# RWKV-7 / HGRN2 mixer layer on one core: another order of the input projections, a longer hold on whole-array visits, and residual tiles asked for later

## The chip, the cores and the metric

The kernel runs on one core of one Trainium2 chip. The metric is the device time in microseconds (us) of one execution, here a median over several runs. The engines that matter are TensorE (PE, with its weight loads shown as PEld), VectorE (DVE), ScalarE (ACT), GpSimd (POOL), and SyncE (SP), whose queue issues nearly all the transfers between HBM and the on-chip memory.

## The reference

One layer on 512 frames of 2048 channels. One input projection feeds two groups of heads: an RWKV-7 recurrence (16 heads of 64) and an HGRN2 gated linear recurrence (8 heads of 128). Their gated outputs are joined, go through one output projection, and the residual is added before a layer norm. Cut to what matters:

```python
proj = jnp.einsum('btd,dc->btc', h, w_in[l])              # 512 x 2048 by 2048 x 8320
rw = _token_shift(proj[..., :RWKV_COLS], shift_mu[l])     # r, k, v, z, and two ranks of 64
hg = proj[..., RWKV_COLS:]                                # q, f, i, z of HGRN2
# RWKV-7, frame by frame, per head (S is 64 x 64):
S = S * w_t + (S @ a_t) b_t^T + v_t k_t^T;   o_t = S @ r_t
# HGRN2, chunks of 64 frames, per head (S is 128 x 128):
S = S * exp(b_last) + k_dec^T i;   o = att(q, k, decay) i + (q * exp(b)) S
y = jnp.einsum('btc,cd->btd', jnp.concatenate([o_rwkv, o_hgrn], -1), w_out[l])
h = _layer_norm(ALPHA * h + y, ln_w[l], ln_b[l])
```

All is float32, and the output has to be float32-like too.

## The kernel before

**Precise matmuls.** Every operand of the two big projections is split into a high and a low part of type fp32r, and each product is made of three matmuls (high by high, high by low, low by high) into the same PSUM bank. This is `three`; its matmuls are the lines L525 of the profile, and L1390 for the first three units. Below, such a matmul of 512 moving columns is called a main matmul. The split of a weight tile `wr` (or `t`, where tiles of that pool hold weights) is one ACT copy (`wh<-wr`) and one DVE subtraction (`wl<-wr,wh`).

**Units.** The input projection is cut into units named by a letter and a number: `w0` (the two ranks), `r`, `k`, `v`, `z` 0 to 7 for RWKV-7 (two heads each), `q`, `f`, `g` 0 to 7 and `i` 0 and 1 for HGRN2 (`g` is its gate). A table, `ORDER`, sets in which order they are computed; `_layout` lays out the weights in the same order. The file holds two tables under that name, and the later one counts.

**The planner.** All other work is written as Python generators that yield operations, each with its engine, reads and writes. While the program is being built, the class `Plan` keeps an estimated clock for every engine. After each main matmul, `pump` goes through its queues of generators, and places an operation in the instruction stream as soon as the estimate says that its inputs will be there. What comes out is a fixed order on each engine; on the chip each engine follows its own order and waits on semaphores. The planner's constants therefore move instructions, and nothing of them runs on the chip.

TensorE does two kinds of work beside the main matmuls, and an interruption of the main stream by such work is called a visit here. A *whole* visit uses the full 128x128 array with float32 operands (the steps of the RWKV scan, `mix<-bd,q` and `mix<-zz,q`, two matmuls each; the outputs of HGRN2 heads; transposes). A *narrow* visit uses parts of the array (16 to 48 matmuls of 32x32 up to 64x128). Each float32 matmul of a visit has two records in the trace. `HOLD` says how long the planner keeps an operation of each kind back, from the moment that it could go, in the hope that a second one joins it; in the last six units (`HURRY`) nothing is held.

**The output projection.** Its first column block (d = 0) runs as rows: for each of 16 k-tiles, four token tiles into the four `main` banks. When those four sums are done, `row_out` adds the residual (`q<-g,main`, DVE), for which `residual` fetches a tile of x into one of four buffers `g` (`g<-x_r`, SP queue). The middle blocks (d = 1 and 2) are then computed by seven *joint passes* of 8 k-tiles and two banks each, a Strassen-like scheme: the first two passes take their weights from `w_all`, later ones partly from sums prepared earlier (`sums_w`, `sums_a`). The weights of a pass come in four loads, two of 512 KB into `wr` and two pairs of 256 KB tiles into `t`. A load into a buffer is issued when the split of what the buffer held is placed, so it waits for that split. The last block (d = 3) follows. The residual tiles of the four blocks stand in one queue, `fetches`, in the order in which `residual` is called: four for d = 0 during the rows, eight for the joint passes, four for d = 3.

Of the kernel before, what the change touches and what calls it, by code (L numbers as in the profile page):

```python
# [39 lines left out]
ORDER = (  # L40
# [3 lines left out]


ORDER = (
# [3 lines left out]


def _order():

    return [(u[0], int(u[1:])) for u in ORDER.split()]
# [10 lines left out]
class Plan:  # L65
# [4 lines left out]

    AFTER = {"pe": 0.2, "act": 0.145, "dve": 0.13, "pool": 0.06, "dma": 0.0, None: 0.1}
    TO_PE = 0.12
    HOLD = {"whole": 0.3, "narrow": 1.0}
    TURN = 0.215
    REST = 1.5
    LEAD = -0.35
# [130 lines left out]
    def worth(self, op, now):  # L207
# [8 lines left out]
        kept = [t for t, o in self.waiting.values() if o.mode[0] == op.mode[0]]  # L216
        if len(kept) == 1 and now < kept[0] + self.HOLD[op.mode[0]]:
            return False
# [44 lines left out]
def mixer_kernel(ctx, tc, head, x_r, w_all, par, up, ln_wb, consts, hmask, out):  # L263
    nc = tc.nc
    pe, sc_e, dve, pool = nc.tensor, nc.scalar, nc.vector, nc.gpsimd
# [9 lines left out]
    def nm(s):  # L275
        uid[0] += 1
        return f"{s}{uid[0]}"
# [5 lines left out]
    plan = Plan({**BUFS, **PBUFS})  # L283
    tags = {}

    def st(tag, shape, dt=F32):
        return spool.tile(shape, dt, tag=tag, name=nm(tag), bufs=BUFS[tag])

    def take(tag, shape=(P, T), dt=F32):

        if not plan.free(tag):
            raise RuntimeError(f"no room: {tag}")
        slot = min(plan.slots[tag])
        plan.slots[tag].remove(slot)
        if tag in PBUFS:
            t = ppool.tile(list(shape), dt, tag=tag, name=nm(tag), bufs=PBUFS[tag])
            plan.banks.add(t.tensor.name)
        else:
            t = st(tag, list(shape), dt)
        name = t.tensor.name  # L300
        plan.busy[name] = (slot[1], None)
        tags[name] = tag
        return t
# [26 lines left out]
    def send(o, i, cost=0.44):  # L330

        nc.sync.dma_start(o, i)
        (to, _), (at, by) = (d.get(ap.tensor.name, (0.0, None)) for d, ap in ((plan.busy, o), (plan.ready, i)))
        plan.clock["sp"] = max(plan.clock["sp"], plan.clock["pe"], to + 0.1, at + 0.1) + cost


    def size(ap):
        n = 1
        for s in ap.shape[1:]:
            n *= s  # L340
        return n
# [160 lines left out]
    def ready(i, home=None):  # L502

        if i < 2 * nload and i not in parts:
            parts[i] = home() if home else tuple(st(t, [P, QT], F32R) for t in ("wh", "wl"))
            if not home:
                ring.append(i)
                before = ring[-1 - BUFS["wh"]] if len(ring) > BUFS["wh"] else -1
                for t in parts[i]:
                    plan.busy[t.tensor.name] = (over.get(before, 0.0), "pe")  # L510

            def run():
                yield from split(*parts[i], raws[i // 2][i % 2])
                whole_parts.add(i)
                if i % 2:
                    load(i // 2 + (2 if i // 2 < joint else 4))

            plan.add(splits, run())

    def three(ps, lh, ll, rh, rl, first, last):  # L520
        n = size(rh)
        for i, (l, r) in enumerate(((lh, rh), (lh, rl), (ll, rh))):
            plan.clock["pe"] += n / 2400 + 0.0145 + plan.turn(("main",))
            plan.mode = ("main",)
            pe.matmul(ps, l, r, start=first and i == 0, stop=last and i == 2)  # L525
            plan.pump()
        if last:
            plan.ready[ps.tensor.name] = plan.busy[ps.tensor.name] = (plan.clock["pe"], "pe")
# [6 lines left out]
    def part(i, width):  # L535

        ready(i)
        for k in range(len(over), min(i, last_parts)):
            over[k] = plan.clock["pe"]
        hi, lo = parts[i]  # L540
        plan.until(lambda: i in whole_parts and by_now(lo))
        return (hi.rearrange("p (k c) -> p k c", c=width), lo.rearrange("p (k c) -> p k c", c=width))

    def main_ps(tags=("main",)):

        def test():
            now = plan.clock["pe"]
            free = [t for t in tags if plan.free(t) and min(plan.slots[t])[1] + 0.15 <= now]
            if not free and plan.free("mix", 3) and sorted(plan.slots["mix"])[0][1] + 0.15 <= now:
                free = ["mix"]  # L550
            return free

        plan.until(test)
        return take(min(test(), key=lambda t: min(plan.slots[t])[1]))
# [891 lines left out]
    asked, whole = [], []  # L1446
# [87 lines left out]
    def union_done(n):  # L1534

        now = plan.clock["pe"]
        for t in {t.tensor.name: t for t in (homes[n, m] for m in range(NPAIRS))}.values():
            plan.busy[t.tensor.name] = (now, "pe")
        if n in ("S2", "S4"):
            drop(*(homes[n, m] for m in range(NPAIRS)))  # L1540
        else:
            drop(homes[n, 0, "ia"], homes[n, 4, "zz"], homes[n, 6, "zz"])
        homes[n, "free"] = True
# [11 lines left out]
    SS = [{} for p in range(NPAIR)]  # L1555

    HURRY = _order()[-6:]
    HS = [{} for _ in range(NHEAD)]
    for name, j in _order()[1:]:
# [195 lines left out]

    xrs = {}

    fetches = plan.queue()

    def residual(t, d):  # L1760
        def run():
            yield lambda: len(whole) == KT and plan.free("g")
            xr = take("g")
            send(xr, x_r[t, :, d * T : d * T + T])
            plan.fetched(xr, 4 * T)
            xrs[t, d] = xr
            now = plan.clock["pe"]
            yield lambda: plan.clock["pe"] > now + (2.0 if d else 0.5)

        plan.add(fetches, run())  # L1770
# [101 lines left out]
    def factor(name, m, i):  # L1872
        sl = slice(i * P, i * P + P)
        if name in ("A11", "A12", "A22"):
            k = korder[2 * m + (name != "A11")]
            sl = slice(T // 2 + i * P, T // 2 + i * P + P) if name == "A22" else sl
            return gh[k][:, sl], gl[k][:, sl]
        plan.until(lambda: (name, m) in unioned and by_now(unioned[name, m][1]))
        hi, lo = unioned[name, m]
        return hi[:, sl], lo[:, sl]  # L1880
# [11 lines left out]
    def home(i):  # L1892
        n = i - single0
        if n < 0:
            if (i - parts0) % 4 < 3:
                return None

            def kept():
                if not fourth:
                    fourth.extend(take("ksq", (P, QT), F32R) for _ in range(2))  # L1900
                for t in fourth:
                    plan.busy[t.tensor.name] = (over.get(i - 4, 0.0), "pe")
                return tuple(fourth)

            return kept
        if n < 7:
            return lambda: tuple(take("t", (P, QT), F32R) for _ in range(2))
        if n < 9:
            def one():
                z = take("zz", (P, 2, QT), F32R)  # L1910
                return z[:, 0], z[:, 1]

            return one
        if n < 11:
            def both():
                if "last" not in homes:
                    homes["last"] = take("ia", (P, 4, QT), F32R)
                return homes["last"][:, 2 * (n - 9)], homes["last"][:, 2 * (n - 9) + 1]

            return both  # L1920
        if n == 11:
            return lambda: tuple(fourth)
        if n == 12:
            return lambda: tuple(take(tag, (P, QT), F32R) for tag in ("pf", "ksq"))

    def prepared(i):

        ready(i, home(i))

    for p, (_, name) in enumerate(PASSES):  # L1930
        pss = []
        for m in range(NPAIRS):
            n = parts0 + p * NPAIRS + m
            hi, lo = part(n, T)
            for i in range(2):
                if m == 0:
                    pss.append(main_ps(banks))
                prepared(n + 1 + 2 * i)
                if i == 0:
                    prepared(n + 2)  # L1940
                three(pss[i], *factor(name, m, i), hi[:, 0], lo[:, 0], m == 0, m == NPAIRS - 1)
                if m == NPAIRS - 1:
                    plan.add(evacs, gather(name, i, pss[i]))
        if name in ("S1", "S2", "S3", "S4"):
            union_done(name)
# [175 lines left out]
```

## Time and profile before

| | |
|---|---|
| median of 3 runs | 1015.25 us (1014.25 to 1015.29) |
| the profiled execution | 1015.2 us, span 1013.3 us |
| granted TensorE clock | 1.000 |
| PE / PEld / DVE / ACT / POOL busy, share of the span | 99% / 82% / 85% / 50% / 4% |
| DMA | 161.74 MB, mean 160 GB/s |

Some rows of the profile show starts and durations of single instructions. Because matmuls are pipelined, a main matmul has a duration of 0.39 us in such a row while the next one starts 0.227 us after it: the distance between starts is what a matmul costs, and the chain of work that ended last gives that distance as the length of a piece divided by its count (x64 in 14.53 us). A number in brackets at the end of a row is the idle time of the engine before it, with what ended it.

### The profile page before, as it was taken

How to read it: one execution, taken by the hardware profiler on the slowest of the kernel's cores; microseconds unless marked ns; L12 is line 12 of the kernel's file. 1: busy time of each engine (PE TensorE's matmuls, PEld its weight loads, DVE VectorE, ACT ScalarE, POOL GpSimd, SP SyncE). 2: the span in 40 equal slices, each digit the busy share in tenths (PEclk: the TensorE clock that was granted, in tenths of full speed). 3: DMA queues.
4: the chain of work that ended last, by engine and by line, in shares of the span. 5: the costliest groups of instructions: out<-in, count | busy, mean ns of one | idle time of the engine just before them, and what ended most of it. 6: DMA issues, size and time to landing. Idle time of an engine off the chain costs nothing.

```text
span 1013.3 us, 18890 instructions
## 1 busy us (share of the span) xinstructions
PE 1006.2 (99%) x7081; PEld 831.2 (82%) x7081; DVE 864.2 (85%) x1894; ACT 507.1 (50%) x963; POOL 43.0 (4%) x78
## 2 busy tenths in 40 slices
PE   9999999999999999999999999999999999999997
PEld 8888888888888888888888888888888888878886
DVE  7688689967898998888989987888999898988867
ACT  5557335345646434544673455636343556466531
POOL 0000000000010001002000010020001001000001
PEclk9999999999999999999999999999999999999999
DMA  9766664442456353235555332346463338797633
GB/s 337 240 215 209 216 225 134 138 136 80 145 145 183 104 150 100 64 100 148 154 172 162 114 91 84 90 139 171 137 186 116 117 104 254 222 308 236 204 126 127
DMA packets 80492, 161.74 MB, mean 160 GB/s; under 512 B 11408, under 2 KB 38288, under 8 KB 80400
## 3 DMA queue, kind: packets, MB, share of 16 engines
q1 hardware_dynamic: 79968, 159.61, 51.5%
q8 instruction: 56, 0.92, 0.4%
q10 hardware_dynamic: 432, 0.92, 0.3%
q14 instruction: 36, 0.29, 0.1%
HBM read 130.48 MB, written 30.02 MB: 158 GB/s over the span
## 4 chain that ended last, share of the span: by engine, by line
PE 99%; DVE 0%; ACT 0%; DVEq 0%; issue 0%
PE main L525 75%; PE mix L354 10%; PE mix L525 9%; PE main L1390 3%; PE main L354 2%; PE mix L1341 0%; PE mix L359 0%; PE main L1984 0%; DVE wl L378 0%; ACT wh L368 0%; DVE inv L391 0%; DVEq L2117 0%; DVE inv L1339 0%
## 5 line engine op out<-in xcount | busy, mean ns | idle before, releaser
L525 PE MATMUL main<-xl,wh 128*128 128x512 f32 x848 | 333.3, 393 | 0.0
L525 PE MATMUL main<-xh,wl 128*128 128x512 f32 x848 | 333.1, 393 | 0.0
L525 PE MATMUL main<-xh,wh 128*128 128x512 f32 x848 | 332.9, 393 | 0.0
L368 ACT ACTIVATE wh<-wr 128x512 fp32r<-128x512 f32 x285 | 177.9, 627 | 168.4 <-PE main L525 118.8
L378 DVE TENSOR_TENSOR wl<-wr,wh 128x512 fp32r<-128x512 f32 x285 | 193.9, 681 | 27.8 <-ACT wh L368 23.9
L525 PEld LDWEIGHTS main<-xh,wl 128*128 128x128 f32 x848 | 159.4, 188 | 32.5
L525 PEld LDWEIGHTS main<-xh,wh 128*128 128x128 f32 x848 | 159.3, 188 | 32.4
L525 PEld LDWEIGHTS main<-xl,wh 128*128 128x128 f32 x848 | 159.3, 188 | 32.2
L525 PE MATMUL main<-wh,xh 128*128 128x512 f32 x194 | 76.1, 392 | 0.0
L378 DVE TENSOR_TENSOR inv<-inv 128x256 f32<-128x256 f32 (+10 forms) x184 | 64.4, 355 | 13.7 <-DMA inv<-w_all 10.3
L525 PE MATMUL main<-wh,xl 128*128 128x512 f32 x194 | 76.0, 392 | 0.0
L525 PE MATMUL main<-wl,xh 128*128 128x512 f32 x194 | 75.9, 391 | 0.0
L525 PEld LDWEIGHTS main<-wh,xh 128*128 128x128 f32 x194 | 36.4, 188 | 8.1 <-DVE t L391 0.5
L525 PEld LDWEIGHTS main<-wl,xh 128*128 128x128 f32 x194 | 36.4, 188 | 7.4
L525 PEld LDWEIGHTS main<-wh,xl 128*128 128x128 f32 x194 | 36.5, 188 | 7.4
L378 DVE TENSOR_TENSOR inv<-inv,inv 64x30 f32<-64x30 f32 (+14 forms) x120 | 38.5, 321 | 2.7
L368 ACT ACTIVATE t<-mix 64x128 f32<-64x128 f32 (+3 forms) x71 | 18.4, 262 | 41.0 <-DVE zz L378 24.0
L378 DVE TENSOR_TENSOR t<-t,tot 128x256 f32<-128x256 f32 x96 | 37.9, 416 | 0.3
L369 ACT ACTIVATE t<-main,om 128x512 f32<-128x512 f32 x33 | 22.2, 685 | 29.7 <-PE main L525 22.7
L391 DVE SCALAR_TENSOR_TENSOR bd<-mix,pc,bd 64x64 f32<-64x64 f32 x112 | 31.7, 283 | 5.3 <-PE mix L354 3.0
L368 ACT ACTIVATE q<-t 128x256 f32<-128x256 f32 (+1 forms) x51 | 21.8, 445 | 24.9 <-DVE t L378 21.4
L369 ACT ACTIVATE t<-main 128x512 f32<-128x512 f32 x31 | 17.9, 594 | 22.8 <-PE main L525 22.6
(320 smaller groups left out, 1614.8 us busy)
## 6 DMA issues: line engine op xcount, KB each, us to landing
wr<-w_all SPq DMA_DIRECT2D x142, 512.0 KB, 3.9
inv<-w_all SPq DMA_DIRECT2D x16, 512.0 KB, 5.1
sums_w<-inv SPq DMA_DIRECT2D x16, 512.0 KB, 5.0
q<-head SPq DMA_DIRECT2D x14, 448.0 KB, 5.8
far<-ksq SPq DMA_DIRECT2D x22, 256.0 KB, 4.0
t<-w_all SPq DMA_DIRECT2D x20, 256.0 KB, 4.5
t<-spill SPq DMA_DIRECT2D x17, 256.0 KB, 3.9
far<-q SPq DMA_DIRECT2D x8, 512.0 KB, 5.0
```

Of the source, the lines that this page charges most:

```text
L354: return Op([("pe", cost, lambda: pe.matmul(o, l, r, start=start, stop=stop, **kw))], [l, r], [o], mode=("narrow", l.shape[0], 32 if m <= ...
L368: return "act", cost, lambda: sc_e.activation(o, i, f, scale=scale)
L369: return "act", cost, lambda: sc_e.activation(o, i, f, scale=scale, bias=bias)
L378: return dve_op([a, b], o, lambda: dve.tensor_tensor(o, a, b, f), base=base or 0.16 if o.shape[0] < P and size(o) == C and o.tensor.name i ...
L391: return dve_op([a, b], o, lambda: dve.scalar_tensor_tensor(o, a, s, b, f1, f2), per=0.00113, base=0.085 if o.shape[0] == P and size(o) > ...
L525: pe.matmul(ps, l, r, start=first and i == 0, stop=last and i == 2)
L1390: pe.matmul(pss[a], *ops, start=k == 0 and low == of == 0, stop=k == KT - 1 and low == 1)
```

## The change

Four edits:

1. A new `ORDER` table behind the others.
2. `HOLD["whole"]` goes from 0.3 to 1.0: outside of the last six units, the planner keeps a whole visit back for up to 1 us, as it did with narrow ones.
3. In `three`, the planner's clock is charged 0.09 for a main matmul that follows a whole visit.
4. The residual tiles of d = 1 and 2 are asked for only when the planner's clock stands 8 us behind the start of the joint passes; until then they were asked for as soon as a buffer `g` was free.

```diff
+ORDER = (
+    "w0 k0 r0 f1 r1 k1 v0 g0 v1 q1 q0 f0 g1 i0 z0 z1 r3 k2 f2 r2 "
...
-    HOLD = {"whole": 0.3, "narrow": 1.0}
+    HOLD = {"whole": 1.0, "narrow": 1.0}
...
     def three(ps, lh, ll, rh, rl, first, last):
         n = size(rh)
         for i, (l, r) in enumerate(((lh, rh), (lh, rl), (ll, rh))):
-            plan.clock["pe"] += n / 2400 + 0.0145 + plan.turn(("main",))
+            plan.clock["pe"] += n / 2400 + 0.0145 + plan.turn(("main",)) + (0.09 if plan.mode[0] == "whole" else 0.0)
...
-    fetches = plan.queue()
+    fetches, began = plan.queue(), []

     def residual(t, d):
         def run():
             yield lambda: len(whole) == KT and plan.free("g")
+            if 0 < d < 3:
+                yield lambda: bool(began) and plan.clock["pe"] > began[0] + 8.0 and plan.free("g")
...
         ready(i, home(i))

+    began.append(plan.clock["pe"])
     for p, (_, name) in enumerate(PASSES):
```

The kernel computes the same things with the same instructions; 5500 matmuls stand on TensorE before and after, of the same kinds. Their order is another one from the fourth unit on. Three places follow. In all of them the number behind a tile's name only tells buffers apart, and the lines of the new kernel lie six further down.

**SP, around the start of the joint passes.** Before, from the first residual tile on (`g` is a residual tile; `wr` and `t` from `w_all` are weights of the first two joint passes):

```order
L332 DMA g_9527<-x_r 128x512
L332 DMA g_9533<-x_r 128x512
L332 DMA g_9550<-x_r 128x512
L332 DMA g_9557<-x_r 128x512
L332 DMA t_9553<-w_all 128x512
L332 DMA t_9554<-w_all 128x512
L332 DMA wr_9582<-w_all 128x1024
L332 DMA t_9574<-w_all 128x512
L332 DMA t_9575<-w_all 128x512
L332 DMA g_9600<-x_r 128x512
L332 DMA wr_9615<-w_all 128x1024
L332 DMA g_9624<-x_r 128x512
```

After, the same stretch of the queue:

```order
L338 DMA t_9539<-w_all 128x512
L338 DMA t_9540<-w_all 128x512
L338 DMA g_9560<-x_r 128x512
L338 DMA wr_9570<-w_all 128x1024
L338 DMA g_9572<-x_r 128x512
L338 DMA t_9543<-w_all 128x512
L338 DMA t_9544<-w_all 128x512
L338 DMA g_9592<-x_r 128x512
L338 DMA g_9603<-x_r 128x512
L338 DMA wr_9612<-w_all 128x1024
L338 DMA t_9539<-w_all 128x512
L338 DMA t_9540<-w_all 128x512
```

The first pair of `t` tiles has moved ahead of all residual tiles, the second pair has two of them ahead of it where it had four, and the first residual tile of the joint passes has gone from the tenth place here to behind the four `t` loads that follow.

**DVE, at the same place.** Before, with `q<-g,main` the residual addition of the d = 0 rows, `wl<-wr,wh` and `ksq<-wr` the splits of the first joint pass (`wl_9539` is its first k-tile, `wl_9577` its second):

```order
L378 TENSOR_TENSOR wl_9539<-wr_9455,wh_9538 128x512
L378 TENSOR_TENSOR t_9525<-t_9526,g_9266 128x256
L378 TENSOR_TENSOR t_9526<-g_9415,t_9525 128x256
L391 SCALAR_TENSOR_TENSOR q_9559<-g_9527,main_8964 128x512
L1732 BN_STATS stats<-q_9559 128x6
L378 TENSOR_TENSOR wl_9577<-wr_9455,wh_9576 128x512
L391 SCALAR_TENSOR_TENSOR q_9561<-g_9533,main_8974 128x512
L391 SCALAR_TENSOR_TENSOR q_9563<-g_9550,main_8986 128x512
L378 TENSOR_TENSOR wl_9593<-wr_9512,wh_9592 128x512
L378 TENSOR_TENSOR ksq_9607<-wr_9512,ksq_9606 128x512
```

After (`wl_9566` is the second k-tile of the first pass, `wl_9585` the third, `ksq_9600` the fourth):

```order
L384 TENSOR_TENSOR wl_9566<-wr_9455,wh_9565 128x512
L384 TENSOR_TENSOR t_9558<-g_9065 128x256
L384 TENSOR_TENSOR t_9558<-t_9559,g_9065 128x256
L384 TENSOR_TENSOR t_9559<-g_9414,t_9558 128x256
L384 TENSOR_TENSOR wl_9585<-wr_9510,wh_9584 128x512
L384 TENSOR_TENSOR t_9589<-tw_9314,t_9589 128x256
L384 TENSOR_TENSOR ksq_9600<-wr_9510,ksq_9599 128x512
L397 SCALAR_TENSOR_TENSOR q_9548<-g_9560,main_8983 128x512
L384 TENSOR_TENSOR wl_9618<-t_9539,wh_9617 128x512
```

The splits of the second to fourth k-tile now stand ahead of the first residual addition, which waits for its tile of x; before, three residual additions stood ahead of the third.

**PE, in the d = 0 rows.** Before, the outputs of the last RWKV scan (`big`) and a visit of the last HGRN2 pair (`q`, `t`) stand together:

```order
L525 MATMUL main_8986<-wh_8940,xl_8897 128x512
L354 MATMUL mix_9017<-zz_7679,big_7306 64x64 x16
L354 MATMUL mix_9018<-zz_8005,big_7306 64x64 x16
L354 MATMUL mix_9069<-q_8173 32x32 x8
L354 MATMUL mix_9069<-q_8174 32x32 x8
L354 MATMUL mix_9069<-t_8055,t_8151 64x64 x4
L354 MATMUL mix_9069<-t_7846,t_7954 64x64 x4
L525 MATMUL main_8995<-wh_8940,xh_8896 128x512
```

After, the outputs stand alone:

```order
L531 MATMUL main_8999<-wh_9036,xh_9078 128x512
L360 MATMUL mix_9142<-zz_7687,big_7266 64x64 x16
L360 MATMUL mix_9143<-zz_8295,big_7266 64x64 x16
L531 MATMUL main_8999<-wl_9037,xh_9078 128x512
L531 MATMUL main_8999<-wh_9036,xl_9079 128x512
```

The other visit now stands ahead, between main matmuls of the last unit. Over the whole program, counted in this way, visits made of whole-array matmuls alone went from 60 to 53. Narrow matmuls of two different steps share a visit in four places before: 32x32 ahead of the 128x32 kind twice, the other way round once, and the one just shown. After, there are three: the first kind once, the second twice.

2 rows, old and new, of the table ORDER are left out of this document.

## Prediction

> **What bounds the kernel now.** I read the chain of work that ended last first, by line:
>
> ```profile
> PE main L525 75%; PE mix L354 10%; PE mix L525 9%; PE main L1390 3%; PE main L354 2%; PE mix L1341 0%; PE mix L359 0%; PE main L1984 0%; DVE wl L378 0%; ACT wh L368 0%; DVE inv L391 0%; DVEq L2117 0%; DVE inv L1339 0%
> ```
>
> Nearly the whole span is TensorE working through its own stream. Next the busy time by stretch (length, then PE, PEld, DVE, ACT, POOL with instruction counts, the clock, the DMA engines' busy share, GB/s), for the projections and for the hand-over from the d = 0 rows to the joint passes:
>
> ```profile
> 40.00:868.00 828.00, 827.88 (x6308) 686.70 (x6307) 719.50 (x1613) 420.17 (x799) 36.62 (x63) 1.00 0.49 144
> 868.00:895.00 27.00, 26.09 (x113) 20.54 (x112) 22.68 (x48) 13.55 (x30) 0.00 (x0) 1.00 0.82 258
> ```
>
> In the projections TensorE is never idle for longer than the pipeline hides, the clock is full, and the matmuls are the same after the change. So a new order can win there only what visits cost beside their matmuls, and short waits. The second stretch is different: TensorE idles, and the DMA engines are 0.82 busy against 0.49. Its chain, with the price of a main matmul first (14.53 / 64 = 0.227 us):
>
> ```profile
> 87.17 14.53 PE main L525 x64
> ...
> 880.58 8.41 PE mix L525 x36
> 888.99 0.63 ACT wh L368
> ...
> 889.64 0.70 DVE wl L378
> ...
> 890.39 4.76 PE mix L525 x19
> ```
>
> From 880.58 to 895.15 are 14.57 us. The chain names 36 + 19 matmuls, and one more (by high, low) runs between the ACT and the DVE piece: 56 x 0.227 = 12.71. So 1.86 us are lost, nearly all where TensorE stands still for the split of the seventh k-tile of the first pass. The instructions behind it, by start:
>
> ```profile
> 879.61 0.69 DVE L391 SCALAR_TENSOR_TENSOR q<-g,main 128x512 f32<-128x512 f32 x1 [1.39 <-DMA g<-x_r]
> 880.94 0.67 DVE L378 TENSOR_TENSOR wl<-wr,wh 128x512 fp32r<-128x512 f32 x1
> 881.64 0.33 SPq L332 DMA_DIRECT2D wr<-w_all  x1
> 882.06 0.86 SPq L332 DMA_DIRECT2D t<-w_all  x2
> 888.98 0.63 ACT L368 ACTIVATE wh<-t 128x512 fp32r<-128x512 f32 x1 [2.75 <-PE mix L525]
> ```
>
> DVE waits 1.39 us for a residual tile and only then does the split of the second k-tile (880.94 to 881.61). The load `wr<-w_all` on SP needs that split (its buffer), and goes at 881.64; the pair `t<-w_all` stands behind it on SP and goes at 882.06. ACT starts on that pair at 888.98, 6.9 us later. The row names TensorE as what ended the wait, but TensorE itself was waiting; that it was the landing is my inference, and these rows of the issues, the first over the whole run, the second for 874 to 884 us, support it:
>
> ```profile
> t<-w_all SPq DMA_DIRECT2D x20, 256.0 KB, 4.5
> ...
> t<-w_all SPq DMA_DIRECT2D x4, 256.0 KB, 6.1
> ```
>
> So the loss has two causes in a row: a load that goes late because DVE's queue stands behind a residual tile, and a slow landing because residual tiles and weights share busy DMA engines.
>
> **The change, part by part.**
>
> *Residual tiles later, and the new place of the splits: -1.86 us.* In the new DVE order the splits of the second to fourth k-tile stand ahead of the first residual addition. That takes away the wait of 1.39 us and the 1.33 us from the addition's start to the split's (880.94 - 879.61), so up to 2.7 us; ACT's half of the split has to come first, so I count 2.0. The `wr` load moves by as much, and the second `t` pair behind it too, less one residual tile that now stands between them on SP (half of 0.86 us): issued at 880.5. With even the slow 6.1 us it lands at 886.6; ACT and DVE take 0.63 + 0.70 to split it, 887.9, and TensorE needs it at 888.8 (36 matmuls behind 880.58): 0.9 us of slack where there was a deficit, and 2.5 with the usual 4.5 us. Fewer bytes stand ahead of it, too: two residual tiles instead of four, and the first `t` pair goes earlier. Ends: all 1.86 us gained; nothing gained. I take the whole. The joint passes' own residual tiles come later; up to the fourth pass a sum leaves its PSUM bank before the residual is added, so only DVE's queue can wait for them.
>
> *Whole visits, 60 to 53.* A visit of two matmuls (four records), one of ten, and the main matmuls around them:
>
> ```profile
> 243.94 1.81 PE main L525 x8
> 245.76 0.44 PE mix L354 x4
> 246.20 1.60 PE main L525 x7
> ...
> 466.24 2.23 PE mix L354 x20
> 468.47 2.77 PE mix L525 x12
> ```
>
> Without 15 x 0.227 = 3.405 for the main matmuls, the short visit costs 3.85 - 3.405 = 0.445, and the long one 2.23 + 2.77 - 12 x 0.227 = 2.28, or 0.455 for every two matmuls. A fixed cost of coming and going would make the short one dearer by the matmul; it does not, and by the rounding of these rows it lies between -0.01 and 0.01 us. Seven visits fewer bring -0.07 to +0.07, taken 0. The 0.09 us that the planner is now charged for each return is not in this trace. The longer hold alone costs TensorE nothing, since main matmuls fill the time; what it delays is a rival.
>
> *Narrow visits parted: +0.28.* Alone, a 32x32 visit, a 128x32 visit, and both in one in either order:
>
> ```profile
> 391.86 0.68 PE mix L354 x50
> 392.54 2.72 PE main L525 x11
> 395.26 1.50 PE mix L354 x114
> 396.76 4.10 PE main L525 x17
> ...
> 148.12 0.82 PE mix L354 x64
> 148.94 8.15 PE main L525 x35
> ...
> 778.91 1.62 PE mix L354 x114
> 780.53 4.31 PE main L525 x18
> ```
>
> Without 0.227 for each main matmul behind them: 0.90 and 1.03 alone, 1.74 with 32x32 first (saves 0.19), 1.84 the other way round (saves 0.09). The third kind of sharing, scan outputs with the 128x32 and 128x64 kinds, is priced by these:
>
> ```profile
> 278.12 2.02 PE mix L354 x64
> 280.13 18.81 PE main L525 x82
> ...
> 173.10 1.00 PE mix L354 x48
> 174.10 26.07 PE main L525 x114
> ...
> 832.40 3.02 PE mix L354 x112
> 835.42 14.74 PE main L525 x64
> ```
>
> 2.22 and 1.19 alone, 3.23 together: saves 0.18. Before: 2 x 0.19 + 0.09 + 0.18 = 0.65. After: 0.19 + 2 x 0.09 = 0.37. The change loses 0.28.
>
> *Other waits of the old order: 0.* The new order cannot keep the places of the old short waits, but it has new ones of its own. The largest before lie around 828 us, where a visit waits for DVE and the rows then wait for their fourth PSUM bank:
>
> ```profile
> 827.10 0.62 PE mix L354 x4
> 827.72 1.17 PE main L525 x5
> ...
> 828.92 2.11 PE main L525 x8
> ```
>
> The visit: 0.62 - 0.44 = 0.18. Behind it, from 827.72 to 831.03 are 3.31 us for 13 main matmuls, 0.36 more than 13 x 0.227. Together 0.54 us; with the shorter ones elsewhere I put them at 0.9 (an estimate: two thirds as much again). The same planner with the same margins made the new order, so I expect as much again: ends -0.9 and +0.9, taken 0.
>
> *Sum.* 1015.2 (the profiled execution: its span of 1013.3 and 1.9 around it; 0.05 below the median of the runs) - 1.86 + 0 + 0.28 + 0 = 1013.6 us. 0.2% is 2.0 us, about what a measurement of this kernel can tell from no change, so "faster" begins at 1013.2.
>
> **Rivals.**
>
> 1. *The wait stays, or moves to the third pass.* Four residual tiles (1 MB) now go while `sums_w` and `sums_a` tiles are fetched for it.
>
> ```profile
> 894.18 0.33 SPq L332 DMA_DIRECT2D wr<-sums_w  x1
> ...
> wr<-sums_w SPq DMA_DIRECT2D x8, 512.0 KB, 4.6
> ...
> 904.22 22.09 PE main L525 x96
> ```
>
> The pass's first weights go at 894.18, land 4.6 us later and are split in 1.3, 900.1; the pass starts at 904.22, so 4.1 us are spare. All of 1 MB ahead of them at 258 GB/s takes 4.1 us: just covered, if it all lay ahead. The Trainium skill ("DMA: Bandwidth & Descriptors", section "Issuing engines are not separate DMA queues") says that transfers run on the same 16 engines and interleave, whichever engine starts them: by that, deferring tiles moves load and removes none, and this kernel could lose in pass three what it wins in pass one. The row of 0.82 busy engines agrees that they are shared; that the slack is used up, no row shows. With the gain gone: 1015.2 + 0.28 = 1015.5.
>
> 2. *The scattered waits go as well.* In the new order two visits instead of one, and the same nine main matmuls, stand between the last unit's end and the first matmul into the fourth bank, which gives its evacuation 0.45 us more. Against it: nothing in the trace says that the other waits do not come again. 1013.6 - 0.9 = 1012.7.
>
> 3. *Slower: the hold stretches the RWKV scans.* Between the two visits of a scan step the old order has 7 main matmuls (as in the row of 246.20), the new one 10 in the unhurried groups: 0.68 us for each of 7 steps, 4.8 us for a scan. If the buffers of a scan then come free so late that the next group's evacuation stops and the four main banks fill, TensorE waits for up to that long once: 1013.6 + 4.8 = 1018.4. It decides from 3.7 us of new waits on (1017.3). Against it: the last group's visits are not held, and the new order has its last scan's outputs 69 matmuls later but the last transposes of HGRN2 31 and 18 earlier, ahead of the rows that need them.
>
> 4. *A return from a whole visit does cost the 0.09.* Seven fewer: -0.63, so 1013.0. The visits above speak against it.
>
> **How the numbers follow.** My forecast's case (the wait of the first pass gone, other waits about as before) has 0.60; its own range is 1012.9 to 1014.4, a third of it under 1013.2. Rival 1 has 0.15 (same), rival 2 0.17 and rival 4 0.02 (faster), rival 3 0.06 (slower by more than 2.0 us in 0.05). Faster: 0.20 + 0.17 + 0.02 = 0.39. Slower 0.05. Same 0.56. The range goes from rival 2 less 0.2 (1012.5) up to 1015.0, where rival 1 begins if a part of the wait comes back: that leaves out most of rival 1, rival 3, and little else.
>
> **What would show it.** In the chain of the new kernel, no ACT or DVE piece between 880 and 895 us; the second `t` pair issued about 2 us earlier; DVE without an idle stretch on `g<-x_r` ahead of the second split. Visits of two matmuls still at 0.45 us. The 32x32 and 128x32 visits alone at 0.90 and 1.03. The forecast is wrong if such a piece stands in the third pass, or if TensorE's busy share in the projections falls below 827.9 of 828 us.

## The result, and the profile after

The changed kernel is slower: 1030.8 us median of 4 runs (1026.9 to 1033.2) against 1015.3 (1014.3 to 1016.1) for the kernel before, a ratio of 1.015 with a 95% interval of 1.013 to 1.017. That is 15.5 us, where I had forecast a gain of 1.7. The profiled execution is the longest of the four: 1033.24 us, with a span of 1031.5, 18.2 more than before. The runs also scatter over 6.3 us, those of the kernel before over 1.8. The lines of `mixer_kernel` stand six lower in the changed file: L531 here is L525 before, L360 is L354, L384 is L378, L397 is L391.

Two lines answer the first two of before. The first is the page's chain by line, the second the busy time by stretch (length, then PE, PEld, DVE, ACT, POOL, the clock, the DMA engines' busy share, GB/s):

```profile
PE main L531 62%; PE mix L360 9%; PE mix L531 5%; PE main L1396 3%; DMA inv<-w_all 3%; DVE wl L384 2%; DMA sums_w<-inv 2%; PE main L360 1%; DMA wr<-w_all 1%; DVE inv L384 1%; DVE t L384 1%; DMA g<-x_r 1%; DMA t<-far 1%; DMA spill<-g 0%; DMA t<-spill 0%
...
40.00:868.00 828.00, 818.17 (x6233) 675.60 (x6232) 711.74 (x1611) 405.29 (x760) 34.82 (x61) 0.99 0.46 137
```

The chain had hardly anything in it but TensorE; now 8% of it are transfers, `inv<-w_all` first. TensorE's busy time in the projections is 818.2 of 828 us instead of 827.9, and the clock is no longer full throughout. This is the sign that the prediction named for being wrong.

To size the loss I took the starts of neighbouring matmuls of 512 columns (0.227 us apart when nothing waits) and summed what was over it, from 20 us on. Gaps of 0.35 us and more ("holes" below) hold 15.3 us, against 2.6 before; main matmuls at 0.427 us (half speed) add 3.8, against none. Together 16.5 us more, of 18.2. Two places hold 11 us of it. The first, at 95 us, by start on PE and on DVE, then the transfers issued from 86 to 98 us (KB each, median us to landing):

```profile
95.02 0.39 PE L531 MATMUL main<-xl,wh 128*128 128x512 f32 x1
98.92 0.79 PE L531 MATMUL main<-xh,wl 128*128 128x512 f32 x1 [3.51 <-DVE wl L384]
```

```profile
96.91 1.34 DVE L384 TENSOR_TENSOR inv<-inv 128x256 f32<-128x256 f32 x3 [6.03 <-DMA inv<-w_all]
98.17 0.69 DVE L384 TENSOR_TENSOR wl<-wr,wh 128x512 fp32r<-128x512 f32 x1
```

```profile
wr<-w_all SPq DMA_DIRECT2D x1, 512.0 KB, 5.8
q<-far SPq DMA_DIRECT2D x4, 128.0 KB, 6.4
inv<-w_all SPq DMA_DIRECT2D x1, 512.0 KB, 7.0
sums_w<-inv SPq DMA_DIRECT2D x1, 512.0 KB, 7.8
```

TensorE stands because it needs the low half `wl` of a weight tile. That split is an easy 0.69 us on DVE, and its operands had been there; but it stands in DVE's queue behind three subtractions of `weight_sums`, and these wait 6.0 us for their `inv` tile. The tile took 7.0 us to land, behind five other transfers issued in the 2.6 us ahead of it and with a store right behind. The planner reckons 1.8 us behind the transfer itself (`fetched`), and counts there neither the four `q<-far` tiles nor the store into `sums_w`.

When TensorE went on, it ran at half speed. Two stretches behind the two longest holes (the number behind POOL's count is the granted clock):

```profile
99.00:104.60 5.60, 5.60 (x13) 4.37 (x14) 3.84 (x8) 0.99 (x2) 0.00 (x0) 0.50 0.80 240
...
170.00:173.40 3.40, 3.40 (x10) 2.67 (x9) 3.37 (x3) 0.90 (x2) 0.00 (x0) 0.52 0.04 16
```

So the place at 95 us costs 3.9 us of idling and 13 x 0.2 us of slow matmuls. The second place, at 166 us, has the same beginning; its chain:

```profile
156.20 5.75 DMA inv<-w_all
...
163.69 0.69 DVE wl L384
...
166.55 0.68 DVE wl L384
...
168.16 0.69 DVE t L397
...
168.88 3.42 PE main L531 x9
```

It costs 2.9 us and seven slow matmuls. The waits of DVE on these tiles in the whole run, before and after (us in total, times, longest):

```profile
DVE inv L378 <- DMA inv<-w_all: 10.3, 6, 3.9
```

```profile
DVE inv L384 <- DMA inv<-w_all: 20.5, 7, 6.0
```

The row of before was there to be read: DVE already stood 3.9 us behind such a tile, and nothing of it reached TensorE. I had looked at TensorE's waits, not at this near miss.

The rest of the loss is spread: 1.4 us at 140 and 1.3 at 335, 0.8 at 727 and at 794, and 1.4 at 886 in the rows just ahead of the joint passes, where an output of the last heads, turned by way of DRAM (`far`), comes back late (chain):

```profile
875.41 4.44 DMA wr<-w_all
879.87 6.17 DMA t<-far
...
886.16 0.88 DVE g L397 x3
```

### The profile page after: what moved, and what is told of

The parts are those of the page before. It is cut to its first block, busy times and chain, and to the rows that moved or that the text cites. A ratio compares the mean times of both kernels' runs of the same rounds, so it can differ in the third digit from the quotient of the medians.

```text
span 1031.5 us, 18880 instructions
## 1 busy us (share of the span) xinstructions
PE 1013.1 (98%) x7081; PEld 832.6 (81%) x7081; DVE 871.6 (85%) x1922; ACT 500.3 (49%) x937; POOL 46.7 (5%) x78
## 4 chain that ended last, share of the span: by engine, by line
PE 82%; DMA 8%; DVE 7%; issue 1%; ACT 1%; POOL 0%; SPq 0%; DVEq 0%; POOLq 0%; ACTq 0%
PE main L531 62%; PE mix L360 9%; PE mix L531 5%; PE main L1396 3%; DMA inv<-w_all 3%; DVE wl L384 2%; DMA sums_w<-inv 2%; PE main L360 1%; DMA wr<-w_all 1%; DVE inv L384 1%; DVE t L384 1%; DMA g<-x_r 1%; DMA t<-far 1%; DMA spill<-g 0%; DMA t<-spill 0%
## 5 line engine op out<-in xcount | busy, mean ns | idle before, releaser
L531 PE MATMUL main<-xh,wl 128*128 128x512 f32 x864 | 340.1, 394 | 3.5 <-DVE wl L384 3.5
L531 PE MATMUL main<-xl,wh 128*128 128x512 f32 x864 | 340.8, 394 | 0.0
L531 PE MATMUL main<-xh,wh 128*128 128x512 f32 x864 | 340.2, 394 | 0.0
L384 DVE TENSOR_TENSOR wl<-wr,wh 128x512 fp32r<-128x512 f32 x285 | 194.0, 681 | 19.4 <-ACT wh L374 17.6
L531 PEld LDWEIGHTS main<-xh,wl 128*128 128x128 f32 x864 | 163.0, 189 | 37.0 <-DVE wl L384 3.9
L531 PEld LDWEIGHTS main<-xl,wh 128*128 128x128 f32 x864 | 163.0, 189 | 33.6
L531 PEld LDWEIGHTS main<-xh,wh 128*128 128x128 f32 x864 | 163.0, 189 | 33.6
L384 DVE TENSOR_TENSOR inv<-inv 128x256 f32<-128x256 f32 (+10 forms) x184 | 65.0, 355 | 24.2 <-DMA inv<-w_all 20.5
L531 PE MATMUL main<-wh,xh 128*128 128x512 f32 x210 | 82.8, 394 | 2.6 <-DVE t L397 2.3
L531 PE MATMUL main<-wh,xl 128*128 128x512 f32 x210 | 83.2, 396 | 1.2 <-DVE xl L384 1.2
L531 PE MATMUL main<-wl,xh 128*128 128x512 f32 x210 | 83.1, 396 | 0.2 <-DVE wl L384 0.2
L531 PEld LDWEIGHTS main<-wh,xh 128*128 128x128 f32 x210 | 39.9, 190 | 11.5 <-DVE t L397 2.8
L531 PEld LDWEIGHTS main<-wh,xl 128*128 128x128 f32 x210 | 39.9, 190 | 10.3 <-DVE xl L384 2.3
L531 PEld LDWEIGHTS main<-wl,xh 128*128 128x128 f32 x210 | 39.7, 189 | 8.9 <-DVE wl L384 0.7
L384 DVE TENSOR_TENSOR inv<-inv,inv 64x30 f32<-64x30 f32 (+14 forms) x120 | 38.4, 320 | 2.4
L397 DVE SCALAR_TENSOR_TENSOR bd<-mix,pc,bd 64x64 f32<-64x64 f32 x112 | 31.7, 283 | 8.6 <-PE mix L360 6.6
L384 DVE TENSOR_TENSOR t<-t,tot 128x256 f32<-128x256 f32 x96 | 37.7, 417 | 0.1
L374 ACT ACTIVATE t<-mix 64x128 f32<-64x128 f32 (+3 forms) x63 | 16.5, 263 | 38.3 <-DVE zz L384 23.6
```

The costliest lines, as they stand in the source:

```text
L374: return "act", cost, lambda: sc_e.activation(o, i, f, scale=scale)
L384: return dve_op([a, b], o, lambda: dve.tensor_tensor(o, a, b, f), base=base or 0.16 if o.shape[0] < P and size(o) == C and o.tensor.name i ...
L397: return dve_op([a, b], o, lambda: dve.scalar_tensor_tensor(o, a, s, b, f1, f2), per=0.00113, base=0.085 if o.shape[0] == P and size(o) > ...
```

## The experiments

"Over before" is always the difference to the runs of the kernel before that were timed beside it (medians of 1014.0 to 1015.3 us). One more number stands beside the times. Where nothing can be issued, the planner's `until` adds 0.05 us to its TensorE clock; the sum of these additions while a kernel is built is what the plan itself knows of idling. It is 1.6 us for the kernel before and 1.6 us for the changed one, so the 15.5 us are nothing that the plan could see.

**Is it DVE behind `inv<-w_all`?** Instructions stay in the order of the changed kernel on all engines.

```diff
-  yield tt(w[:, o], w[:, a], w[:, b], ALU.subtract)
+  yield Op([("dve", same cost, subtract of xh[0], xl[0] into aside)], [w], [w])
```

> The changed kernel, every instruction of it in its place on every engine; only the 64 subtractions of weight_sums read two resident tiles and write a small byte tile instead of working in `inv`, so that DVE never waits for `inv<-w_all` there (sums_w then holds the weight blocks themselves: the outputs of those passes are left wrong). Theory A (DVE stood behind late `inv<-w_all`, TensorE ran dry, and its matmuls went at half speed after it): the holes of 3.9 us at 95 us and 2.7 us at 166 us and the 22 matmuls at 0.427 us are gone; 10 to 12 us less than the changed kernel's 1030.8: 1019 to 1021. Rival B (the longer hold stretches the scans): nothing changes at 95 and 166 us, 1030 to 1031. Rival C (the transfers as a whole are late there, and DVE would have met the next late tile anyway): 2 to 5 us less, 1026 to 1029.

Measured: 1023.2 us, ratio 1.008 (1.006 to 1.010): 8.2 over before instead of 15.5. The stretch around the first hole, and what is left, by chain:

```profile
90.00:100.00 10.00, 10.00 (x45) 8.26 (x45) 7.98 (x15) 8.70 (x14) 0.00 (x0) 1.00 0.91 253
```

```profile
126.33 6.64 DMA wr<-w_all
...
317.72 5.16 DMA t<-spill
...
866.97 5.95 DMA t<-far
```

Both holes are gone, with their slow matmuls: 7.3 us by the medians. That is less than theory A's 10 to 12, and 1023.2 lies above its 1019 to 1021; I had sized it on the longest of the changed kernel's runs. What is left are holes of 0.8 to 1.4 us (at 133, 323, 781, 873 us), three of them behind other tiles that took 5 to 7 us to land.

**Do the same transfers stretch the others?** The edit above, and the 16 loads and 16 stores of `weight_sums` not issued; then the same in the kernel before.

> The changed kernel, the plan untouched, with the subtractions of weight_sums cut loose as in the first of these runs and also its 16 loads of `w_all` and 16 stores into sums_w left out (16 MB of 162 MB; the joint passes read other blocks of `w_all` instead: wrong values). Theory A (what the plan does not know are landings stretched by the other transfers): the hole of 0.9 us at 133 us, behind a `wr` tile that took 6.6 us to land, goes too, those at 323, 781 and 873 us stay, since the left-out transfers lie ahead of them: 1021 to 1023 after 1023.2. If the rest of the loss (8 us) also hangs on these transfers: 1015 to 1019. If the new order is slower in itself, whatever lands when: 1023.

> The same leaving out in the kernel before, its plan untouched: the control for it. It has no hole of 0.5 us ahead of 880 us, so 1012 to 1015.

Measured: 1020.5 us, ratio 1.006 (1.005 to 1.008), 6.5 over before; and 1013.8 for the control, ratio 1.000 (0.999 to 1.001). The hole at 133 us is gone, the others stay, as theory A said (the time lies half a microsecond under its 1021 to 1023):

```profile
316.80 4.52 DMA t<-spill
...
866.56 6.16 DMA t<-far
```

So of 15.5 us, 7.3 are DVE standing behind `inv`. Another 1.7 may be what its transfers do to other tiles; the intervals of these two kernels overlap (1.006 to 1.010 and 1.005 to 1.008), so only the hole itself shows it. The other 6.5 stay: the landings at 323 and 873 us, the joint passes, an operand at 781 us that DVE comes to late, and lesser ones. These are located in the traces; no run takes them out. The same leaving out is worth nothing in the kernel before: there all this was hidden.

**Which part of the change?** The new order does not stand alone: without the hold of 1.0 or without the charge the planner finds no next step. First the change without its residual part, then all but the new order.

> The changed kernel without the residual edit: new order, hold of 1.0 and the charge of 0.09. Theory A: the holes at 95, 140, 166 and 335 us stay, since nothing of the residual edit acts ahead of about 870 us; the wait of the first joint pass is 1 to 2 us either way; 1029 to 1033. If the residual edit made the loss: 1012 to 1017.

> The kernel before's order of projections, with the hold of 1.0, the charge of 0.09 and the residual edit. Rival B (the hold): the loss stays without the new order, 1024 to 1031. Theory A: what counts is at which places the plan has DVE meet late tiles; the hold moves these places too, so holes may come, but not the ones at 95 and 166 us; 1013 to 1021.

Without the residual part: 1030.4 us, ratio 1.016 (1.014 to 1.017), the holes at 95 and 166 us as before. It is not the residual part. With the old order: 1026.8, ratio 1.012 (1.010 to 1.013), so the loss does not come from the new order alone. But it is another loss: the holes at 95 and 166 us are gone, and one of 7.0 us stands at 876, with 12 slow matmuls behind it. Its chain:

```profile
867.57 5.14 DMA far<-ksq
...
872.79 4.35 DMA t<-far
...
877.15 3.55 DMA t<-far
...
882.53 0.64 ACT xh L368
...
883.21 6.82 PE main L525 x17
```

The outputs of the last heads go through DRAM and back so late that TensorE has nothing else left. This hole the plan knew: its clock stands still for 6.0 us at 873 us (7.6 in all). My expectation for theory A, 1013 to 1021, was too low.

**Hold or charge, or any new plan?** Three edits of one number each, in the kernel before, with its order.

```diff
 # charge alone
+ plan.turn(("main",)) + (0.09 if plan.mode[0] == "whole" else 0.0)
 # hold 0.6
-    HOLD = {"whole": 0.3, "narrow": 1.0}
+    HOLD = {"whole": 0.6, "narrow": 1.0}
 # turn, a control
-    TURN = 0.215
+    TURN = 0.225
```

> The kernel before with the charge of 0.09 us on the first main matmul behind a whole visit, and nothing else. If the loss with the old order (1026.8 with hold and charge together) comes from the hold: 1014 to 1017. If the charge alone brings it: 1023 to 1029. Theory E: anything from 1015 to 1030, with holes at places of its own.

> The kernel before with the hold of whole visits at 0.6 us instead of 0.3, and nothing else (1.0 alone leaves the planner without a next step). If the hold delays the last scan and with it the rows of the output passes (the hole of 7.2 us at 876 us with hold and charge): part of that hole, 1016 to 1024. If not: 1014 to 1016. Theory E: 1015 to 1030 with holes elsewhere.

> A control: the kernel before with the planner's price of a turn between modes at 0.225 us instead of 0.215. Nothing is meant by it but a plan made anew: most matmuls keep their neighbours, some visits slip by a matmul or two. If the plan's quality is that of its rules: 1014.5 to 1016. Theory E: as bad as the others, 1018 to 1030.

Measured: 1019.8 (ratio 1.006, 1.004 to 1.007), 1025.1 (1.011, 1.009 to 1.013) and 1026.7 (1.012, 1.010 to 1.014). The control is as slow as the others: a hundredth of a microsecond in one price, meant for nothing, costs 12 us. Its chain shows where, the rows of the output passes again; behind it stands the busy time of 6 us in that piece:

```profile
860.26 4.95 DMA t<-far
...
870.20 6.98 PE mix L354 x40
```

```profile
869.30:875.30 6.00, 5.98 (x28) 6.00 (x29) 1.39 (x4) 1.05 (x3) 0.00 (x0) 0.50 0.36 112
```

40 records of whole visits take 7.0 us there, where four take 0.44 and 40 would take 4.4. They do not wait among themselves: they come back to back, without main matmuls between them, behind a hole of 3.2 us at 866 us in which TensorE waited for DVE, and the first 6 us of them run at a granted clock of 0.50. Another hole, of 2.6 us, follows at 877. The hold of 0.6 has its hole at 477 us, 6.1 us long. So a new plan by itself can cost this much, without the hold.

**Are short landing estimates the cause, and do later ones cure it?** In the changed kernel two of them were raised, in the kernel before the one that `fetched` takes where none is given.

```diff
 # changed kernel
-            plan.fetched(w, 4 * HALF)
+            plan.fetched(w, 4 * HALF, 5.0)
-                plan.fetched(gated[k], 4 * T, 3.6)
+                plan.fetched(gated[k], 4 * T, 7.0)
 # kernel before
-    def fetched(self, tile, size, late=1.8):
+    def fetched(self, tile, size, late=3.5):
```

> The changed kernel with two landing estimates of its planner raised: the `w_all` tiles of weight_sums from 1.8 to 5.0 us, the gated rows brought back for the output passes from 3.6 to 7.0 us. The plan moves with them. Theory A (too short landing estimates at these places make the loss): the holes of 3.9 and 2.7 us at 95 and 166 us, with the slow matmuls behind them, and the one of 1.4 us at 886 us are gone; 1014 to 1020. Theory E (any plan made anew meets late tiles at some places, the estimates of two kinds do not decide it): holes of 1 to 7 us elsewhere, 1020 to 1032.

> The kernel before with the planner's landing estimate of fetched tiles at 3.5 us behind the transfer instead of 1.8, old order. The planner's own clock then stands still for 4.0 us in all instead of 1.6. Theory A (what the plan knows of, it hides; holes come where a landing is later than it thinks): before plus some 2 us, 1015 to 1018. Theory E (any plan made anew has holes that the chip alone shows): 1019 to 1031.

The first: 1122.5 us, ratio 1.107 (1.105 to 1.109), a miss for every theory. The plan's clock stands still for 131.8 us in it: with these estimates the new order of projections has stretches in which nothing can be issued at all. (The hole at 886 us would not have been reached by them: it hangs on `t<-far`, which has an estimate of its own in `turned`.) Two of its stretches, with TensorE busy for 4.0 of 21 and 1.6 of 18 us:

```profile
575.00:596.00 21.00, 3.98 (x8) 2.02 (x9) 18.22 (x33) 14.37 (x21) 2.40 (x4) 0.51 0.38 120
963.00:981.00 18.00, 1.55 (x5) 0.85 (x5) 8.43 (x18) 4.05 (x7) 3.24 (x2) 0.64 0.54 164
```

The second: 1017.2 us, ratio 1.002 (1.001 to 1.003), as theory A said. That plan too is made anew throughout, and loses 2.9 us, of which its clock knows 2.4. So "any new plan is bad" is wrong as well. That later estimates cure the new order is not shown.

**A control with a small move.**

```diff
-    def send(o, i, cost=0.44):
+    def send(o, i, cost=0.45):
```

> A second control: the kernel before with the planner's price of one issue on SP at 0.45 us instead of 0.44. Its plan differs from before in an eighth of TensorE's rows and a sixth of SP's, and its own clock stands still as little as before (1.6 us). Theory A and its planner's idle time: 1014 to 1017. Theory E: up to 1030.

Measured: 1014.3 us, ratio 1.000 (0.999 to 1.001). The kernels with plans of their own, together:

| kernel | plan's clock stands still, us | over before, us |
|---|---|---|
| before | 1.6 | 0 |
| send at 0.45, old order | 1.6 | 0.0 |
| residual part alone, old order | 1.6 | -0.1 |
| charge alone, old order | 2.1 | 5.5 |
| later landings, old order | 4.0 | 2.9 |
| hold and charge and residual part, old order | 7.6 | 11.8 |
| turn at 0.225, old order | 8.4 | 12.4 |
| hold 0.6, old order | 11.2 | 10.8 |
| changed, without the residual part | 1.6 | 15.5 |
| changed | 1.6 | 15.5 |
| changed, two landings later | 131.8 | 108.2 |

How much of a loss the plan knows differs: with the old order 9.6 of 10.8 us with the hold of 0.6, about half with hold, charge and residual part together (6.0 of 11.8) and with the turn (6.8 of 12.4), but 0.5 of 5.5 with the charge alone. The new order repairs the plan (7.6 back to 1.6 us) and puts DVE behind late tiles instead.

**Moving the subtractions off DVE.** To have the gain of the first experiment in a kernel that computes everything, the subtractions were issued on POOL at their places, in both kernels.

```diff
-  yield tt(w[:, o], w[:, a], w[:, b], ALU.subtract)
+  yield Op([("dve", same cost, pool.tensor_tensor(..., ALU.subtract))], [w], [w])
```

> The changed kernel with the 64 subtractions of weight_sums issued on POOL instead of DVE, every one at its planned place, the plan itself untouched (it still books them on DVE); nothing is left out. Theory A (DVE in its order stood behind late `inv<-w_all`): as when those subtractions were cut loose (1023.2), 1020 to 1025, the holes at 95 and 166 us gone. Rival F (POOL then holds up the sums, its norms or SP's stores, or slows DVE beside it): 1026 to 1033.

> The kernel before with the same move to POOL, its plan untouched. Its DVE waited 10.3 us for `inv<-w_all` with no hole in TensorE, so theory A gives at most the 1 us of small holes ahead of 180 us: 1013.5 to 1015, same. Rival F: POOL late, 1016 to 1020.

Measured: 1030.5 us (ratio 1.016, 1.014 to 1.017) and 1018.2 (1.003, 1.002 to 1.005): rival F, no gain in the one and 3.9 us lost in the other. The hole at 95 us is gone, but the one at 166 us stays (2.0 us, at 164 now): DVE no longer waits for `inv` ahead of it, but its own tensor_tensors there are stretched beside POOL (two of 128x256 take 1.82 us instead of 0.75). And there are new holes, 2.5 us at 56 to 61 and 2.6 at 110. At 50 us, first the changed kernel, then the one with POOL:

```profile
50.95 0.67 DVE L384 TENSOR_TENSOR wl<-wr,wh 128x512 fp32r<-128x512 f32 x1
51.53 1.37 DVE L413 TENSOR_TENSOR pf<-t 32x512 f32<-32x512 f32 x2
```

```profile
51.11 1.16 DVE L384 TENSOR_TENSOR wl<-wr,wh 128x512 fp32r<-128x512 f32 x1
52.20 2.36 DVE L413 TENSOR_TENSOR pf<-t 32x512 f32<-32x512 f32 x2
```

```profile
49.27 3.60 POOL L1334 TENSOR_TENSOR inv<-inv 128x256 f32<-128x256 f32 x3
53.24 4.19 POOL L1334 TENSOR_TENSOR inv<-inv 128x256 f32<-128x256 f32 x4 [0.38 <-DMA inv<-w_all]
```

While POOL subtracts, these instructions of DVE take 1.7 times as long.

**The residual part alone**, in the kernel before.

> The kernel before with the residual edit alone. By the prediction: the wait of 1.86 us in the first joint pass goes, 1013.4 (ratio 0.9982). Rival D (seen in the changed kernel, where 1.3 us of waits remain in the first passes): the wait stays for the most part, behind the second pair of t tiles, 1014.5 to 1015.3.

Measured: 1014.8 us, ratio 1.000 (0.999 to 1.001): nothing gained, within 0.9 us. The chain of its first pass:

```profile
879.08 3.25 DMA g<-x_r
...
882.38 0.67 DVE wl L378
...
883.06 0.33 SPq L332
...
883.48 6.09 DMA t<-w_all
...
889.68 0.64 ACT wh L368
```

The old sequence, step by step: DVE stands behind a residual tile, its split goes at 882.38, the `wr` load that needs the split's buffer at 883.06, the `t` pair behind it, 6.1 us of landing, ACT. SP's queue shows why nothing moved:

```profile
876.50 3.40 SPq L332 DMA_DIRECT2D g<-x_r  x4
880.00 0.85 SPq L332 DMA_DIRECT2D t<-w_all  x2
...
883.48 0.86 SPq L332 DMA_DIRECT2D t<-w_all  x2
```

The four tiles ahead of the pairs belong to d = 0, and the edit does not touch them. The tiles that it does hold back stood behind the second pair already (the first of them at 882.97 in the kernel before, its pair at 882.06).

No version here beats the kernel before; of those run, two equal it (send at 0.45, residual part alone).

## Why the prediction was wrong

*The step of the prediction that failed* is the term "Other waits of the old order", taken as 0 with ends of -0.9 and +0.9 us because "the same planner with the same margins made the new order, so I expect as much again". In the plan that holds to the decimal (1.6 us of idling in both). On the chip the term measured about +15: 15.3 us of holes and 3.8 of slow matmuls where there had been 2.6 and none. About half of it, 7.3 us, is shown by leaving out: DVE in its order behind late `inv<-w_all`. The margins are estimates of when tiles land, and where the new order meets a tile that lands after 6 or 7 us, DVE's queue hands the wait on. The ends of that term should have come from the slack of DVE's waits on transfers (10.3 us in the old order, none of it visible on TensorE), not from the waits that TensorE showed.

*The term of -1.86 us* measured about 0 alone (1014.8 against 1015.0; the wait stays), and alone the edit moves neither splits nor pairs. Their new places come with the rest of the change: the changed kernel without the residual part has the same sequence on SP (a pair, one tile, `wr`, one tile, a pair). So I had credited the residual edit with a sequence that comes without it. The step that failed inside this term is that the second `t` pair would go 2 us earlier. In the changed kernel the DVE order was as I had read it, yet the pair did not move against the pass. The pass's first matmul, SP's issues and ACT's split:

```profile
899.13 0.39 PE L531 MATMUL mix<-wh,xh 128*128 128x512 f32 x1
```

```profile
899.71 0.33 SPq L338 DMA_DIRECT2D wr<-w_all  x1
...
900.57 0.90 SPq L338 DMA_DIRECT2D t<-w_all  x2
```

```profile
906.48 0.63 ACT L374 ACTIVATE wh<-t 128x512 fp32r<-128x512 f32 x1 [3.67 <-DMA t<-w_all]
```

The pair goes 1.44 us behind the pass's start, as before (882.06 - 880.58 = 1.48): other work of DVE now stands ahead of the split at 899.0, late itself through the hole at 886 us. Landing takes 5.9 us. By the starts of its 48 matmuls the first pass now loses 0.5 us instead of 1.7, but the second loses 0.9 instead of 0.1: most of the wait has gone there. Rival 1 was right that the wait stays; the third pass, which it named, loses nothing, as before. Rival 1 rests on the Trainium skill ("DMA: Bandwidth & Descriptors", section "Issuing engines are not separate DMA queues"), that transfers interleave on the same 16 engines. The landings of 5.9 to 6.1 us in these passes are in line with that, where the median of such tiles over the whole run is 4.1 (4.5 before); no run shows the sharing by itself.

*The visits* were right where the trace shows them. The 128x32 kind alone, with the 35 main matmuls behind it, and a visit of two matmuls, in the changed kernel's chain:

```profile
796.13 0.82 PE mix L360 x64
796.95 8.16 PE main L531 x35
...
844.31 0.45 PE mix L360 x4
```

The first costs 8.98 - 35 x 0.227 = 1.03 us again, the second 0.45.

*Rival 3* named the hold and the scans' buffers. The stretch came: from the first to the last step's matmul the three scans under the hold take 43.6, 45.2 and 44.3 us after and 39.7, 37.7 and 40.6 before, which is 3.7 to 7.5 more, and the last one, not held, 37.5 and 36.7. What did not come is the wait: no hole stands at the end of a scan, at 285, 487, 676 or 857 us. So its direction was right and its path was not the one that cost time here. A stage which comes late can make TensorE stand, though: in the old order the hold and the charge did that to the last rows (7.0 us at 876 us), which the new order cured. *Rivals 2 and 4* ended on the wrong side.

What stays open: whether another plan of the new order would keep its waits hidden. Only two plans of it that do not idle of themselves were run, and they are nearly the same. The 6.5 us that stay without the sums are located, but not tested. And the holes of the runs with hold 0.6 and with the charge alone were not followed to a single cause.

## What to carry to other kernels

Where a planner writes the order of everything, a changed price is a new draw of all the waits: cost the edit's terms, but take the range from how far the planner's estimates lie from the measured landings, and from the waits of in-order engines that stay hidden today. A wait of 4 us on DVE that TensorE does not feel is no proof of safety; it says how close the next order is to a hole. When a plan is searched anew, what its clock says of idling is a sieve (the plans that idle 7 us and more by themselves were 11 us slower or worse), but a plan without idling has still to be timed.

## What the runs showed of the hardware

A short hole in TensorE's work can halve its clock afterwards. Measured from start to start of two matmuls, holes of 2.30, 2.52, 2.73, 2.84, 3.90, 4.04, 6.35 and 7.24 us were followed by 5 to 13 matmuls at 0.427 us instead of 0.227, beginning 0.6 to 1.2 us after the restart. Holes of 2.26, 2.45 and 2.74 us were not, nor any below 2.2 that stood alone (one of 1.91 us was, 1 us behind another of 0.95, in the run with two later landings). The same place can go either way: the hole at 166 us was 2.73 us long in the changed kernel, with seven slow matmuls behind it, and 2.74 us without the residual part, with none. The hole of 3.9 us at 95 us so cost 6.5. The Trainium skill ("TensorE: Matmul & The Clock Gate", Part 1) gives 1.2 GHz after an idle window of about 3.4 us that runs freely. The two speeds agree with the granted clock of 0.50 here, but holes well under 3.4 us were enough at some places; there the measurement decides.

POOL's tensor_tensor on SBUF tiles stretched DVE's from 0.67 to 1.16 us. The Trainium skill ("SBUF — State Buffer", section "Who interferes with whom") has a DVE instruction that reads two SBUF tiles contend with a POOL instruction that reads SBUF, over a shared pair of ports; the `wl` split reads two. The trace agrees that they disturb each other. A tensor_scalar of one tile was stretched as well, from 0.54 to 0.95 us.
